# Chunked latent attention on one core: rope scores as two 128-row products instead of three 64-row ones

## The chip, the core and the metric

The kernel runs on one core of a Trainium2 chip. The metric is the device time of one execution in microseconds (us); less is better. Three runs of the kernel before took 1628.82, 1629.12 and 1631.48 us (median 1629.12). Engines are named as in the profile: PE is TensorE, PEld its weight loads, DVE VectorE, ACT ScalarE, POOL GpSimd, SP SyncE. L12 is line 12 of the kernel file.

## The reference

Two transformer blocks in float32 on 512 tokens of width 1024. The first block has an mLSTM layer and then a layer with latent attention; the second block is a pooling and differential attention layer with cross attention and an MLP. The change lies in the latent attention of the first block, 8 heads, cut to what matters:

```python
q = rmsnorm((rmsnorm(q_lat) @ w_q_up).reshape(b, s, 8, 192), q_gain)   # 128 nope + 64 rope columns
q = concat([q[..., :128], rope(q[..., 128:], positions)])
for j in range(4):                                   # blocks of 128 queries
    sc = einsum("bqhd,bkhd->bhqk", q[:, 128*j:128*j+128], k[:, :128*(j+1)]) * 192 ** -0.5
    sc = where(k_chunk <= q_chunk, sc, -inf)         # chunks of 64
    p = softmax(sc)
    out[j] = einsum("bhqk,bkhd->bqhd", p, v[:, :128*(j+1)])
```

The rope part of k (64 columns) is the same for all heads; the scale of q and the per-head scale of k are applied after the products.

## The kernel before, in words

Every float32 operand of a matmul is kept as two float32r tiles, hi and lo (`split`: ACT rounds, DVE subtracts, L534 to L540), and a product is three matmuls, hi by hi, hi by lo and lo by hi (`mm3`, L518). Weights come in slabs by SP's DMA and are split in four pieces each by an ACT and a DVE instruction (L285, L286; scaled ones L292, L293).

The program is a list of units. A unit's matmuls are emitted first; what follows a product (its `post`) is emitted when the next unit begins (`flush`, L451), ahead of which or behind which pieces of the weight slabs are put out: two when a slab begins, one or two for each unit after. All engines run in the order in which the units emit. So the order of units is the order of every engine's queue.

Latent attention handles the 8 heads in four groups of two. `prep(g)` makes the operands of a group: the nope part of k for each head (`kn`), sums of squares (`kss`), the rope part of q of both heads side by side in one 128-row tile (`qr`, rows 0 to 63 head 0, rows 64 to 127 head 1), the nope parts of q (`qn`), the row of k scales through DRAM to a broadcast tile `rkb` (`krow`: a transposition, ACT's copy `rr`, POOL's DMAs `rd` and twice `rkb`), the rotation (`qrot`: two PE products with a permutation, then three DVE operations L1265 to L1267 and a split), sums of squares of q (`qss`: products with one or two columns), and v (`vu`). The rope part of k, `Rk`, is rotated once and lies in both halves of its 128 rows.

`attend(g)` has 8 score tiles (2 heads, 4 query blocks): `f1` makes the scores (three matmuls nope, three matmuls rope with 64 rows, one bf16 mask product, width n = 256, 256, 384, 512), then on DVE the scaled maximum over the row (L1496, which reads `rkb`), `nb` (L1498), on ACT the exponential (L1499). `f2` is DVE's reciprocal and scaling to `e` (L1505, L1506). `f3` transposes e on PE and splits it into `PTh`, `PTl`. `f4` is the product with v (`po`), which reads PTh and PTl of all four blocks of its head, then `ym` and the split into y.

`soft_steps` lays the tiles of a group out in 11 steps: step i has f2 of tile i-1, f1 of tile i, then filling units, then f4 (steps 6 and 10), then f3 of tile i-2. The filling units come from `weave`, which spreads them evenly:

```python
for i, (before, after) in enumerate(steps):
    to = (len(main) * (i + 1)) // len(steps)
    res += before + main[m:to] + after
```

While group g attends, the filling units are `prep(g+1)` without v and the output product of the group before; `vu` follows behind the last step. Group 3 has only output products to fill in. The operands of group 0 are made ahead of everything, in an order written out by hand (L1544).

Of the kernel before, what the change touches and what calls it, by code (L numbers as in the profile page):

```python
# [26 lines left out]
def block_kernel(ctx: ExitStack, tc: tile.TileContext, A: dict, out: bass.AP, stop=None):  # L27
# [1225 lines left out]
        split(h, l, ps, scale=gain)  # L1253
        return ps, h, l, gain

    def rope_rotate(st, cosT, sinT, dst):
        ps, h, l, gain = st
        pr = bank([128, 512], "rot")
        pe.matmul(out=pr, lhsT=prm, rhs=h, start=True, stop=False)
        pe.matmul(out=pr, lhsT=prm, rhs=l, start=False, stop=True)  # L1260
        a, b = T("ra"), T("rb")
        if gain is None:
            dve.tensor_tensor(out=a, in0=ps, in1=cosT, op=ALU.mult)
        else:
            dve.scalar_tensor_tensor(out=a, in0=ps, scalar=gain, in1=cosT, op0=ALU.mult, op1=ALU.mult)  # L1265
        dve.tensor_tensor(out=b, in0=pr, in1=sinT, op=ALU.mult)
        dve.tensor_tensor(out=a, in0=a, in1=b, op=ALU.add)  # L1267
        split(dst[0], dst[1], a)

    mq1, mz0, mz1 = fmu(*bmq[1]), fmu(*bmz[0]), fmu(*bmz[1])  # L1270
    add(mq1, mem_q_ssq(0), mz0, U(rope_tables), mem_q_ssq(1), mz1)
# [116 lines left out]
    def prep(g):  # L1388
        kvb = w_kv_b[:, 512 * g:512 * g + 512].rearrange("(k p) (h c) -> p k h c", p=128, h=2)
        kkey, vkey = ("kvbk", g), ("kvbv", g)  # L1390
        for key, c in ((kkey, 0), (vkey, 128)):
            slabs[key] = ([(128 * h, kvb[:, :, h, c:c + 128]) for h in range(2)], 2, 256, ("kv_lat_norm", 0))
        qkey = ("qup", g)
        parts = []
        for i in range(2):
            src = b_w_q_up[:, 384 * g + 192 * i:384 * g + 192 * i + 192].rearrange("(k p) c -> p k c", p=128)
            parts += [(128 * i, src[:, :, 0:128]), (256 + 64 * i, src[:, :, 128:192])]
        slabs[qkey] = (parts, 3, 384, ("b_q_lat_norm", 0))

        def kn(h):  # L1400
            def post(ps):
                sq = H["ksq", g, h] = T("sq")
                act.activation(out=sq, in_=ps, func=AF.Square)
                k = H["kn", g, h] = pair(bh.p, [128, 512], "kn", bufs=3)
                split(k[0], k[1], ps, scale=g_nope)

            return fmu(kkey, 128 * h, post, src="cT", nk=2)

        def kss(h):
            def fn():  # L1410
                if h == 0:
                    H["kss", g] = bank([128, 2, 4], "ssk")
                sq = H.pop(("ksq", g, h))
                for tb in range(4):
                    pe.matmul(out=H["kss", g][:, h, tb:tb + 1], lhsT=sq[:, tb * 128:tb * 128 + 128], rhs=ones, start=True, stop=True)
                if h == 1:
                    sk = tiny(8, "fac").rearrange("p (a b) -> p a b", a=2)
                    dve.tensor_tensor(out=sk, in0=H.pop(("kss", g)), in1=S["ssp"].unsqueeze(1).to_broadcast([128, 2, 4]), op=ALU.add)
                    H["rk", g] = rsqrt(sk.rearrange("p a b -> p (a b)"), 8, 1.0 / 192)

            return U(fn)

        def krow():
            pr = bank([8, 128], "rkT")
            pe.transpose(out=pr, in_=H.pop(("rk", g)), identity=ident)
            rr = T("rr")[0:8, 0:128]
            act.copy(out=rr, in_=pr)
            rd = dram.tile([8, 128], F32, tag="rd", name="rd")
            pool.dma_start(out=rd, in_=rr)
            for h in range(2):  # L1430
                rb = H["rb", g, h] = bh.p.tile([128, 512], F32, tag="rkb", name="rkb", bufs=3)
                pool.dma_start(out=rb, in_=rd[4 * h:4 * h + 4, :].rearrange("a b -> (a b)").rearrange("(o c) -> o c", o=1).to_broadcast([128, 512]))

        def vu(b):
            def fn(w):
                if b == 0:
                    H["V", g] = pair(bh.p, [128, 4, 256], "V")
                ps = bank([128, 2, 256], "V")
                for i in range(2):
                    tm(ps[:, i], S["cT"], 2 * b + i, w, 0, 256, nk=2)  # L1440
                V = H["V", g]
                return lambda: split(V[0][:, 2 * b:2 * b + 2, :], V[1][:, 2 * b:2 * b + 2, :], ps)

            return U(fn, vkey)

        def qr_post(ps):
            sq = H["qsq", g] = [T("sq")]
            act.activation(out=sq[0], in_=ps, func=AF.Square)
            H["qrs", g] = rope_split(ps, col("b_q_gain", 1))

        def qrot():
            q = H["qr", g] = pair(bh.p, [128, 512], "qr", bufs=2)
            rope_rotate(H.pop(("qrs", g)), S["cos"], S["sin"], q)

        def qn(h):
            def post(ps):
                sq = T("sq")
                H["qsq", g].append(sq)
                act.activation(out=sq, in_=ps, func=AF.Square)
                q = H["qn", g, h] = pair(bh.p, [128, 512], "qn", bufs=3)  # L1460
                split(q[0], q[1], ps)

            return fmu(qkey, 128 * h, post, src="qlT", nk=3)

        def qss():
            sp = bank([128, 4, 2], "ssq")
            sqs = H.pop(("qsq", g))
            for tb in range(4):
                t = slice(tb * 128, tb * 128 + 128)
                pe.matmul(out=sp[:, tb, :], lhsT=sqs[0][:, t], rhs=blk1, start=True, stop=False)  # L1470
                for h in range(2):
                    pe.matmul(out=sp[:, tb, h:h + 1], lhsT=sqs[1 + h][:, t], rhs=ones, start=False, stop=h == 1)
            H["cq", g] = rsqrt(sp.rearrange("p a b -> p (a b)"), 8, 1.0 / 192, post=192 ** -0.5)

        qr = fmu(qkey, 256, qr_post, src="qlT", nk=3)
        return ([kn(0), kss(0), kn(1), kss(1), qr, qn(0), qn(1), U(krow), U(qrot), U(qss)],
                [vu(0), vu(1)])

    def attend(g):
        s1, s2, s3, s4 = [], [], [], []  # L1480
        for h in range(2):
            hs = slice(64 * h, 64 * h + 64)
            for j in range(4):
                t = slice(128 * j, 128 * j + 128)
                w = 128 * (j + 1)

                def f1(h=h, hs=hs, j=j, t=t, w=w):
                    n = max(w, 256)
                    kn, qn, qr, Rk = H["kn", g, h], H["qn", g, h], H["qr", g], S["Rk"]
                    ps = bank([128, 512], "sc")  # L1490
                    mm3(ps[:, 0:n], (qn[0][:, t], qn[1][:, t]), (kn[0][:, 0:n], kn[1][:, 0:n]), True, False)
                    mm3(ps[:, 0:n], (qr[0][hs, t], qr[1][hs, t]), (Rk[0][hs, 0:n], Rk[1][hs, 0:n]), False, False)
                    pe.matmul(out=ps[:, t], lhsT=idb, rhs=m_chunk, start=False, stop=True)
                    e = T("e")[:, 0:w]
                    mx, nb, sm = (tiny(1, n_) for n_ in ("mx", "nb", "sm"))
                    dve.tensor_tensor_reduce(out=e, in0=ps[:, 0:w], in1=H["rb", g, h][:, 0:w], scale=1.0, scalar=-3e38, op0=ALU.mult, op1=ALU.max, accum_out=mx)  # L1496
                    c = H["cq", g][:, 2 * j + h:2 * j + h + 1]
                    dve.scalar_tensor_tensor(out=nb, in0=mx, scalar=-1.0, in1=c, op0=ALU.mult, op1=ALU.mult)  # L1498
                    act.activation(out=e, in_=e, func=AF.Exp, scale=c, bias=nb, accum_out=sm)  # L1499
                    H["e", h, j] = e, sm  # L1500

                def f2(h=h, j=j):
                    e, sm = H["e", h, j]
                    rc = tiny(1, "rc")
                    dve.reciprocal(out=rc, in_=sm)  # L1505
                    dve.tensor_scalar(out=e, in0=e, scalar1=rc, scalar2=None, op0=ALU.mult)  # L1506

                def f3(h=h, j=j):
                    e, _ = H.pop(("e", h, j))
                    pt = bank([128, 4, 128], "pt")  # L1510
                    for k in range(j + 1):
                        pe.transpose(out=pt[:, k, :], in_=e[:, 128 * k:128 * k + 128], identity=ident)
                    hi, lo = (pt_view(i, j) for i in range(2))
                    split(hi, lo, pt[:, 0:j + 1, :])

                s1.append(U(f1))
                s2.append(U(f2, early=True))
                s3.append(U(f3))
# [22 lines left out]

    preps = [prep(g) for g in range(4)]
    add(U(open_bh))
    add([preps[0][0][i] for i in (0, 2, 1, 4, 3, 5, 6, 7, 8, 9)], preps[0][1])  # L1544
    for g in range(4):
        m = outproj(f"oB{g - 1}", b_w_out, 2 * (g - 1), 2, slots=((g - 1) % 2,)) if g else []
        if g < 3:
# [689 lines left out]
```

## Time and profile before

| | us |
|---|---|
| three runs | 1628.82, 1629.12, 1631.48 |
| the profiled execution, its own time | 1630.76 |
| its span from first to last instruction | 1629.0 |
| PE busy | 1559.9 (96%) |
| PE weight loads busy | 1354.0 (83%) |
| DVE busy | 1071.3 (66%) |
| ACT busy | 743.3 (46%) |
| POOL busy | 312.5 (19%) |
| first score tile of group 0, last mask product of group 3 | from 662.5, 829.3 |

Busy time of PE counts matmuls from start to a modelled end, and matmuls overlap; so what a matmul costs is read from the distance between the starts of two. The latent attention, with the making of its first operands, lies between 645 and 844 us of the span.

### The profile page before, as it was taken

To read this page: it belongs to the slowest core of one execution; us is meant where nothing else is said; L and a number is where in the kernel's file an instruction comes from. 1 tells how busy PE (TensorE), PEld (TensorE's weight loads), DVE (VectorE), ACT (ScalarE), POOL (GpSimd) and SP (SyncE) were. 2 spreads that over 40 slices of the span, in tenths; PEclk is the share of its full clock that TensorE was granted. 3 is DMA by queue.
4 is the path that set the end of the run, shared out by engine and by line. 5 is a ranking of instruction groups with operands and counts; after the bars stand their busy time and mean duration, and the time that the engine had idled before them with its cause. 6 is when DMAs were issued, how large, how long until landed. Compare 5 with 4: busy or idle time off the path is not lost. (4 is left out here: it accounts for less than half of the span.)

```text
span 1629.0 us, 24253 instructions
## 1 busy us (share of the span) xinstructions
PE 1559.9 (96%) x9385; PEld 1354.0 (83%) x9385; DVE 1071.3 (66%) x1980; ACT 743.3 (46%) x1538; POOL 312.5 (19%) x570
## 2 busy tenths in 40 slices
PE   6999999999999999999989999989999999999996
PEld 6889898988788888778869877868878889898986
DVE  6567646565685563667777555577456579686968
ACT  5344424333465544445544333455333463636353
POOL 4100000000030100211211000012100265555552
PEclk9999999999999999999999999999999999999998
DMA  8422223221332221212324331233312224141411
GB/s 265 140 78 70 87 78 90 67 92 65 129 112 83 91 78 35 92 35 67 124 72 148 116 118 52 73 109 117 99 70 73 76 85 156 52 156 52 142 53 52
DMA packets 134795, 152.75 MB, mean 94 GB/s; under 512 B 7616, under 2 KB 120024, under 8 KB 134680
## 3 DMA queue, kind: packets, MB, share of 16 engines
q1 hardware_dynamic: 131800, 143.58, 27.7%
q0 software_dynamic: 2304, 6.57, 1.4%
q8 instruction: 74, 1.21, 0.3%
q10 hardware_dynamic: 576, 1.05, 0.2%
q14 instruction: 41, 0.34, 0.1%
HBM read 144.88 MB, written 6.31 MB: 93 GB/s over the span
## 5 line engine op out<-in xcount | busy, mean ns | idle before, releaser
L520 PE MATMUL fm<-xth,whi 128*128 128x512 f32 (+1 forms) x824 | 307.3, 373 | 1.0 <-ACT whi L285 0.8
L521 PE MATMUL fm<-xtl,whi 128*128 128x512 f32 (+1 forms) x824 | 305.9, 371 | 1.5 <-DVE xtl L537 1.5
L522 PE MATMUL fm<-xth,wlo 128*128 128x512 f32 (+1 forms) x824 | 305.0, 370 | 0.1
L286 DVE TENSOR_TENSOR wlo<-wraw,whi 128x512 fp32r<-128x512 f32 (+2 forms) x324 | 206.3, 680 | 32.8 <-ACT whi L285 23.3
L285 ACT ACTIVATE whi<-wraw 128x512 fp32r<-128x512 f32 (+2 forms) x324 | 182.7, 619 | 38.8 <-PE op L522 23.3
L521 PEld LDWEIGHTS fm<-xtl,whi 128*128 128x128 f32 x824 | 156.0, 189 | 28.8 <-DVE xtl L537 2.5
L520 PEld LDWEIGHTS fm<-xth,whi 128*128 128x128 f32 x824 | 155.9, 189 | 28.4 <-ACT whi L285 1.0
L522 PEld LDWEIGHTS fm<-xth,wlo 128*128 128x128 f32 x824 | 155.7, 189 | 27.9 <-DVE wlo L286 0.5
L547 POOL TENSOR_TENSOR rsx<-rsy 128x1 f32<-128x1 f32 (+2 forms) x49 | 15.1, 307 | 753.8 <-DVE rsy L546 707.7
L520 PE MATMUL tm<-whi,xth 128*128 128x256 f32 x416 | 116.4, 280 | 0.0
L521 PE MATMUL tm<-wlo,xth 128*128 128x256 f32 x416 | 115.8, 278 | 0.0
L522 PE MATMUL tm<-whi,xtl 128*128 128x256 f32 x416 | 115.7, 278 | 0.0
L669 DVE TENSOR_TENSOR xall<-op,xall 128x512 f32<-128x512 f32 x120 | 81.7, 686 | 47.3 <-PE op L522 47.0
L522 PE MATMUL dn<-whi,ffgl 128*128 128x256 f32 x296 | 82.8, 280 | 0.0
L521 PE MATMUL dn<-wlo,ffgh 128*128 128x256 f32 x296 | 82.7, 279 | 0.0
L520 PE MATMUL dn<-whi,ffgh 128*128 128x256 f32 x296 | 82.6, 279 | 0.0
L521 PEld LDWEIGHTS tm<-wlo,xth 128*128 128x128 f32 x416 | 78.7, 189 | 0.2
L520 PEld LDWEIGHTS tm<-whi,xth 128*128 128x128 f32 x416 | 78.7, 189 | 0.2
L522 PEld LDWEIGHTS tm<-whi,xtl 128*128 128x128 f32 x416 | 78.7, 189 | 0.0
L520 PE MATMUL op<-whi,y0h 128*128 128x512 f32 x160 | 66.8, 417 | 0.0
L522 PE MATMUL op<-whi,y0l 128*128 128x512 f32 x160 | 64.0, 400 | 0.0
L521 PE MATMUL op<-wlo,y0h 128*128 128x512 f32 x160 | 63.8, 399 | 0.0
(590 smaller groups left out, 4038.5 us busy)
## 6 DMA issues: line engine op xcount, KB each, us to landing
wraw<-in_a_w_in_dram SPq DMA_DIRECT2D x23, 1024.0 KB
wraw<-in_w_down_dram SPq DMA_DIRECT2D x19, 512.0 KB
wraw<-in_mem_w_kv_dram SPq DMA_DIRECT2D x8, 1024.0 KB
wraw<-in_b_w_in_dram SPq DMA_DIRECT2D x8, 1024.0 KB
wraw<-in_w_ckv_dram SPq DMA_DIRECT2D x8, 1024.0 KB
wraw<-in_w_in_dram SPq DMA_DIRECT2D x8, 1024.0 KB
wx<-in_w_down_dram SPq DMA_DIRECT2D x13, 512.0 KB
wraw<-in_a_w_out_dram SPq DMA_DIRECT2D x6, 1024.0 KB
```

Of the source, the lines that this page charges most:

```text
L285: act.activation(out=hi[:, s], in_=t[:, s], func=AF.Copy)
L286: dve.tensor_tensor(out=lo[:, s], in0=t[:, s], in1=f(hi)[:, s], op=ALU.subtract)
L520: pe.matmul(out=ps, lhsT=lh, rhs=rh, start=first, stop=False)
L521: pe.matmul(out=ps, lhsT=lh, rhs=rl, start=False, stop=False)
L522: pe.matmul(out=ps, lhsT=ll, rhs=rh, start=False, stop=last)
L547: eng.tensor_tensor(out=x, in0=y, in1=y, op=ALU.mult)
L669: return lambda: dve.tensor_tensor(out=xs[tb][h], in0=ps, in1=xs[tb][h], op=ALU.add)
```

## The change

The three 64-row rope products of a score tile become two of 128 rows. For a head h, `qr[h]` is now one 128-row tile that holds the hi part of the head's 64 rope rows in one half and the lo part in the other. Since Rk has the same 64 rows in both halves, one product with Rk hi gives (hi + lo) by hi, and one with Rk lo gives (hi + lo) by lo. The rotation writes its hi part into the tile `rph` and its lo part into the tile `rb`, and a new unit `qmove` copies the four 64-row pieces of a group into the two tiles `qr[0]`, `qr[1]` by four DMAs on ACT's queue (from SBUF to SBUF, 64 rows of 2 KB each, 128 KB).

`qmove` is one more unit at the end of each `prep`. So groups 1 and 2 spread 19 filling units over 11 steps in place of 18, group 0 spreads 7 over its last 5 steps in place of 6, and the list written by hand for the first operands has the rotation ahead of the second nope part of q, and `krow` behind `qmove`.

```diff
-    def rope_rotate(st, cosT, sinT, dst):
+    def rope_rotate(st, cosT, sinT, dst=None):
         ps, h, l, gain = st
         pr = bank([128, 512], "rot")
         pe.matmul(out=pr, lhsT=prm, rhs=h, start=True, stop=False)
         pe.matmul(out=pr, lhsT=prm, rhs=l, start=False, stop=True)
-        a, b = T("ra"), T("rb")
+        a, bt = T("ra"), T("rb", F32R)
+        b = f(bt)
...
         dve.tensor_tensor(out=a, in0=a, in1=b, op=ALU.add)
+        dst = dst or (h, bt)
         split(dst[0], dst[1], a)
+        return dst
...
         def qrot():
-            q = H["qr", g] = pair(bh.p, [128, 512], "qr", bufs=2)
-            rope_rotate(H.pop(("qrs", g)), S["cos"], S["sin"], q)
+            H["qrp", g] = rope_rotate(H.pop(("qrs", g)), S["cos"], S["sin"])
+
+        def qmove():
+            hl = H.pop(("qrp", g))
+            q = H["qr", g] = [bh.p.tile([128, 512], F32R, tag=f"qr{h}", name="qr", bufs=2) for h in range(2)]
+            for h in range(2):
+                for i in range(2):
+                    d = 64 * (h ^ i)
+                    nc.scalar.dma_start(out=f(q[h])[d:d + 64, :], in_=f(hl[i])[64 * h:64 * h + 64, :])
...
-        return ([kn(0), kss(0), kn(1), kss(1), qr, qn(0), qn(1), U(krow), U(qrot), U(qss)],
+        return ([kn(0), kss(0), kn(1), kss(1), qr, qn(0), qn(1), U(krow), U(qrot), U(qss), U(qmove)],
                 [vu(0), vu(1)])
...
                     mm3(ps[:, 0:n], (qn[0][:, t], qn[1][:, t]), (kn[0][:, 0:n], kn[1][:, 0:n]), True, False)
-                    mm3(ps[:, 0:n], (qr[0][hs, t], qr[1][hs, t]), (Rk[0][hs, 0:n], Rk[1][hs, 0:n]), False, False)
+                    for r in Rk:
+                        pe.matmul(out=ps[:, 0:n], lhsT=qr[h][:, t], rhs=r[:, 0:n], start=False, stop=False)
                     pe.matmul(out=ps[:, t], lhsT=idb, rhs=m_chunk, start=False, stop=True)
...
-    add([preps[0][0][i] for i in (0, 2, 1, 4, 3, 5, 6, 7, 8, 9)], preps[0][1])
+    add([preps[0][0][i] for i in (0, 2, 1, 4, 3, 5, 8, 6, 10, 7, 9)], preps[0][1])
```

## Rows read from the trace of the kernel before

**Rows 1.** Windows: us, PE, PEld, DVE, ACT, POOL busy, clock, DMA, GB/s
```profile
640.00:840.00 200.00, 193.16 (x1028) 154.84 (x1026) 135.53 (x355) 94.42 (x216) 33.66 (x114) 0.96 0.25 75
706.00:709.00 3.00, 3.00 (x12) 2.81 (x12) 2.27 (x4) 0.63 (x1) 0.80 (x2) 0.50 0.68 178
803.20:844.00 40.80, 36.63 (x183) 28.09 (x182) 29.69 (x82) 17.63 (x43) 10.05 (x30) 0.90 0.36 112
```

**Rows 2.** Timeline of PE in the first score tile: start, us, engine, line, what
```profile
662.73 0.28 PE L522 MATMUL sc<-knh,qnl 128*128 128x256 f32 x1
662.94 0.38 PE L520 MATMUL sc<-Rkh,qrh 64*128 64x256 f32 x1
663.17 0.27 PE L521 MATMUL sc<-Rkl,qrh 64*128 64x256 f32 x1
663.28 0.28 PE L522 MATMUL sc<-Rkh,qrl 64*128 64x256 f32 x1
663.49 0.23 PE L1493 MATMUL sc<-masks,idb 128*128 128x128 bf16 x1
663.53 0.48 PE L520 MATMUL fm<-cTh,whi 128*128 128x512 f32 x1
```

**Rows 3.** Instructions on score tiles: ns min/median/max, first and last start, forms
```profile
L522 PE MATMUL sc<-Rkh,qrl x32: 273/305/393, 663.3 to 829.0; 64*128 64x256 f32 x16, 64*128 64x384 f32 x8, 64*128 64x512 f32 x8
```

**Rows 4.** Timeline of PE at the end of group 1
```profile
748.51 0.39 PE L522 MATMUL fm<-qlTh,wlo 128*128 128x512 f32 x1
...
748.85 0.60 PE L1512 MATMUL pt<-ident,e 128*128 128x128 f32 x4
...
752.36 0.47 PE L520 MATMUL po<-PTh,Vh 128*128 128x512 f32 x1
753.27 0.57 PE L521 MATMUL po<-PTl,Vh 128*128 128x512 f32 x1 [0.44 <-DVE PTl L537]
```

**Rows 5.** Timeline of DVE at the end of group 1
```profile
748.31 0.55 DVE L537 TENSOR_TENSOR PTl<-pt,PTh 128x384 fp32r<-128x384 f32 x1
750.12 0.69 DVE L537 TENSOR_TENSOR qnl<-fm,qnh 128x512 fp32r<-128x512 f32 x1 [1.26 <-ACT qnh L536]
750.73 1.89 DVE L286 TENSOR_TENSOR wlo<-wraw,whi 128x512 fp32r<-128x512 f32 x3
752.53 0.68 DVE L537 TENSOR_TENSOR PTl<-pt,PTh 128x512 fp32r<-128x512 f32 x1
...
753.73 0.74 DVE L1265 SCALAR_TENSOR_TENSOR ra<-fm,cols,cosT 128x512 f32<-128x512 f32 x1
...
757.11 0.16 DVE L567 TENSOR_SCALAR rsv<-ssq 128x8 f32<-128x8 f32 x1
```

**Rows 6.** Timeline of PE at the end of group 0
```profile
701.97 0.63 PE L1512 MATMUL pt<-ident,e 128*128 128x128 f32 x4 [1.53 <-DVE e L1506]
```

**Rows 7.** Timeline ahead of group 0: DVE, ACT, ACT, POOL, DVE, PE
```profile
655.19 0.69 DVE L537 TENSOR_TENSOR qnl<-fm,qnh 128x512 fp32r<-128x512 f32 x1 [1.66 <-ACT qnh L536]
...
656.17 0.60 ACT L1459 ACTIVATE sq<-fm 128x512 f32<-128x512 f32 x1 [1.02 <-PE fm L522]
...
657.94 0.24 ACT L1427 COPY rr<-rkT 8x128 f32<-8x128 f32 x1
...
660.38 1.14 POOL L1432 DMA_DIRECT2D rkb<-rd  x2 [1.32 <-DMA rd<-rr]
...
665.15 0.28 DVE L1496 CUSTOM_DVE_ANT_0 e<-sc,rkb 128x128 f32<-128x128 f32 x1
...
668.27 0.51 PE L521 MATMUL op<-wlo,y1h 128*128 128x512 f32 x1 [0.23 <-DVE wlo L286]
```

**Rows 8.** DMA issues, 640 to 662.5: count, KB each, us to landing
```profile
rkb<-rd POOLq DMA_DIRECT2D x2, 256.0 KB, 4.3
```

**Rows 9.** DMA issues of the last line of the kernel: ns minimum, median, maximum
```profile
L2158 ACTq DMA_DIRECT2D out_dram<-xall x4: 343/410/464, 1622.4 to 1624.6; - x4
```

**Rows 10.** Timeline of PE at the end of group 3
```profile
836.19 1.11 PE L1512 MATMUL pt<-ident,e 128*128 128x128 f32 x4 [2.54 <-DVE e L1506]
```

More of the change, by code (lines that the diff above doesn't have):

```diff
@@ L1481, in attend @@
         for h in range(2):
-            hs = slice(64 * h, 64 * h + 64)
             for j in range(4):
@@ L1485, in attend, with f1 @@
                 w = 128 * (j + 1)
-                def f1(h=h, hs=hs, j=j, t=t, w=w):
+                def f1(h=h, j=j, t=t, w=w):
                     n = max(w, 256)
```

## The prediction

> **What bounds the kernel now.** I read the windows first: in the stretch that the change touches, PE is busy 193 of 200 us and DVE 136 [rows 1], so PE is the bound on average, but the last 41 us (group 3) are not like that: PE is idle there for 4.2 us and granted 0.90 of its clock. Then the timeline of PE for one score tile, because a product's price is the distance between starts. Then, at the ends of the groups, the timelines of PE and DVE side by side, because the change moves the rotation there; and last the way of the k scales ahead of group 0. The reader is to see that PE gains something in every tile, that at the group ends DVE's queue ends last, and that the one queue that gets new work (ACT's) stands in the way of group 0's first softmax.
>
> **Score tiles.** Two neighbouring rope products start 0.11 us apart (663.17 to 663.28). But the first starts 0.21 after the last nope product, the second 0.23 after the first, and the mask product 0.21 after the third [rows 2]. So three of the steps cost about 0.1 us more than the work; all three lie where the row count goes from 128 to 64 or back, or just behind it. With 128 rows throughout I take every step at 0.115: from the last nope product to the unit behind the mask 0.39 us (three steps and the mask's 0.04) in place of 0.80, a saving of 0.41 for 256 columns. A 512-column product is 0.12 longer than a 256-column one, a 384-column one about half of that [rows 3]; so 16 tiles save 0.41, 8 save 0.47, 8 save 0.53: 14.6 us for 32 tiles, 3.64 a group.
>
> Here a rule speaks against me. The rows show the 0.1 us steps at each change of the row count. The Trainium skill (TensorE: Matmul & The Clock Gate, section Why this matters for your kernels) says that a single product over few rows takes the same time as one over 128, which leaves only the third product as a gain. By it the saving would be 32 steps of 0.11 to 0.23, 4.9 us; by the rows it is 14.6. I take the rows, and keep the rule as a rival.
>
> **Group 3 keeps nothing.** It has little to fill in, and PE waits there for softmax results, 2.54 us before its last transpositions [rows 10]. Its chain runs from DVE's maximum over ACT's exponential to DVE again; shorter score products lengthen PE's waits. I take 0 of its 3.64 (bounds 0 and -3.64). So the tiles are worth -10.9 in groups 0 to 2.
>
> **The rotation ahead of the last transpositions.** With one more unit, the spread puts `qrot` into step 9 and `qss`, `qmove` into step 10. The transpositions of tile 7 come at the end of step 9. So the rotation, which stood behind them, now stands ahead of them on all three engines: DVE's PTl of tile 7 waits behind ra, rb, the sum, ACT's hi and DVE's lo. And the value product of step 10 needs PTl. From ra to the operation behind the lo part DVE needs 757.11 - 753.73 = 3.38 us, an ACT turn included [rows 5].
>
> Group 1, from the end A of the second nope part of q (748.75, one step of 0.24 after 748.51 [rows 4]). Before: DVE's split of it at A+1.37, three weight pieces (0.60 each), PTl at A+3.8, second value product at 753.27, A+4.5. After: the spread puts both nope parts into step 8, ahead of the transpositions of tile 6. DVE then has behind A: the split (A+1.37 to A+1.98), four weight pieces (2.4) and PTl of tile 6 (0.47), so ra at A+4.8 and PTl of tile 7 at A+8.2; with its 0.65 and PE's start the second value product comes at A+8.9. PE itself would be there at A+3.9 (3.5 from the transpositions to the value product, rotation included [rows 4], and 0.35 for those of tile 6 and the row of k scales): it waits some 5 us. A lies 0.24 earlier, as tile 6's transpositions now follow it. Loss 8.9 - 4.5 - 0.24 = 4.1. Group 2 has the same units: 4.1. In group 0 the four weight pieces and tile 6 already stood ahead of PTl, so only the 3.4 are added; the wait of 1.53 us for e [rows 6] comes from DVE and ACT too and gives nothing back. Sum 11.6. Bounds: if DVE came to ra as soon as the rotation product is there, the chain of 4.1 would stand against 3.0 of PE work (the 3.5 without the rotation), 1.1 less what PE waits now, 1.5 for three groups; 13.5 if the pieces are dearer.
>
> **The four moves.** An issue on ACT costs 0.41 us [rows 9], 1.64 for four, 16 in all. At the group ends ACT has nothing urgent behind them (y and v come later). They land 4.3 us after issue if they behave like the 256 KB broadcasts [rows 8]; from the wait's end PE has the rest of the value products, 24 v products and three nope products, 38 steps of 0.115 at least, 4.4 us, and the issue comes 0.7 before that. This just covers it: 0, bounds 0 and 1.5 a group. The tiles rph and rb are held until the moves land; they are reused 8 allocations later, in the next group's first tiles: 0 while those 4.4 us hold.
>
> **Ahead of group 0.** Now rr, the first link to `rkb`, stands behind the moves on ACT. DVE splits the first nope part at 655.19 [rows 7]; ra follows 0.6 later, 655.8, ACT's hi 2.1 later (ra, rb and the sum), 657.9, then the square of the second nope part at 658.45, then as before 1.77 to where rr stood (656.17 to 657.94), and 1.64 for the moves: rr at 661.9, 3.9 late. POOL's DMAs move with it: `rkb` issued at 664.3 instead of 660.38, landed at 668.6 [rows 8], when DVE's first maximum started at 665.15. Behind this maximum stand on DVE the weight pieces for which PE already waits at 668.27 [rows 7]. So PE goes on about 3.3 us later than before, and the 0.8 that it saved in two tiles are swallowed: +4.1 against the tiles' sum. `qss` also waits for that square, under the same wait. Bounds: -0.4 (the landing hidden, and `krow` no longer waiting for POOL) and 6.
>
> **Clock.** Behind the waits at the group ends PE already runs at half clock (0.50 from 706 to 709) and loses 1.7 us in 3.4; those falls stay. New waits ahead of group 0 may bring one more: +0.7, bounds -3 and 5.
>
> Sum: -10.9 + 11.6 + 4.1 + 0.7 = +5.5. The profiled execution took 1630.76 us, 1.64 above the median of the runs, so 1636.3 on its own scale and 1634.6 on that of the median.
>
> **Rivals.** (A) Faster: DVE reaches the rotation without delay, so the ends cost 1.5 and not 11.6. This decides between gain and loss: up to a start of ra about 1.4 us behind the rotation product instead of 4, the tiles win. Then -10.9 + 1.5 + 4.1 + 0.7 = -4.6: 1624.5; with `rkb` hidden too, 1620. For it: DVE is busy only 136 of 200 us. Against: its queue is in order, with four weight pieces ahead. 0.22. (B) No change: `rkb` is hidden, -0.4 in place of 4.1, and the ends cost as forecast: +1.0, 1630. For it: some slack in the landing. Against: DVE took the first maximum 0.5 us after the landing reckoned by these rows. 0.16. (C) Moves land late and the clock falls for longer: 1.5 in each of three groups and 2 more for the clock, +12, 1641. The Trainium skill (the same page, section HAM oscillation) says that pauses between bursts of products bring the half clock back, and the trace agrees with 0.50 behind such an end. 0.08. (D) The row change is not what costs the 0.1 us steps, so the change does not do what it says: the 24 tiles of three groups give one product each, 0.11, 0.17 or 0.23 by width, 3.7 in place of 10.9: +12.7, 1641.8. The rule on few rows above would have it so. Against: rows 2. 0.06. The forecast has 0.48, its own range 1631 to 1639.
>
> **Numbers.** 0.2% (3.3 us) is about what a measurement can tell. Faster: A with 0.21, the lower edge of B and of the forecast 0.03: 0.24. Same: most of B (0.12) and the forecast's lower part (0.05): 0.17. Slower: 0.59. The range 1622.5 to 1640.5 leaves out the far part of A, and most of C and D.
>
> **What would show it.** Right: rope products at the common step, no 0.2 us starts; at the ends of groups 0 to 2 the L1265 to L1267 operations ahead of the 512-wide PTl, and PE waiting 3 us or more for PTh or PTl at a po product; the first L1496 at 668 or later. Wrong: po products that start without such a wait, a first L1496 near 665, or score tiles whose first rope product still starts late.

## The result, and the profile after

The changed kernel is slower: 1638.76 us (1638.33 to 1643.89, 4 runs) against 1630.30 us (1628.82 to 1632.17, 4 runs), ratio 1.0059 with a 95% interval of 1.0035 to 1.0082. Run again beside two of the experiments it took 1639.65 against 1631.44, ratio 1.0050 (1.0035 to 1.0065). The forecast was 1634.6 with a range of 1622.5 to 1640.5, and slower as the likeliest.

The execution that was profiled first took 1643.89 us, 5.1 over the slowest of the three others. So most rows below are of the second trace, taken when the kernel ran again (1640.04 us, 9.3 over the profiled execution of before); the first one serves where the two differ. Their largest difference in the stretch of the change is 2.9 us ahead of group 0.

First the page of the second trace, its span and busy times:

```profile
span 1638.3 us, 24225 instructions
...
PE 1552.4 (95%) x9353; PEld 1354.1 (83%) x9353; DVE 1072.9 (65%) x1980; ACT 742.5 (45%) x1538; POOL 312.0 (19%) x570
```

PE has 32 products fewer and is busy 7.5 us less (1559.9 before), and still the end is 9.3 us later: the change gave work back and added waiting. The window of [rows 1] and the stretch ahead of group 0, second trace; the last line is that stretch in the first trace:

```profile
640.00:840.00 200.00, 179.56 (x973) 150.20 (x972) 126.14 (x331) 88.62 (x200) 29.03 (x100) 0.92 0.29 84
...
655.00:675.00 20.00, 17.37 (x96) 14.53 (x96) 11.06 (x27) 8.66 (x18) 6.62 (x23) 0.91 0.45 134
...
655.00:675.00 20.00, 17.92 (x89) 16.19 (x87) 8.49 (x20) 7.29 (x16) 5.95 (x23) 0.74 0.43 125
```

PE is now idle for 20.4 of 200 us, where it was idle for 6.8, and its granted clock fell from 0.96 to 0.92. What it waits for is told by the view of waits of PE, 640 to 860 (engine, operation, line, released by: us in total, times, longest); the first fence is before, the second the changed kernel's second trace:

```profile
PE pt L1512 <- DVE e L1506: 4.6, 3, 2.5
PE po L520 <- ACT PTh L536: 0.7, 1, 0.7
```

```profile
PE po L520 <- ACT PTh L536: 11.8, 4, 4.0
PE pt L1524 <- DVE e L1518: 9.1, 7, 2.5
PE ssq L1484 <- ACT sq L1471: 2.1, 1, 2.1
```

The value products wait for PTh, 11.8 us in place of 0.7; the transpositions wait twice as long for e; a wait for a square is new; none is for a moved tile qr. Now the score tile that answers to [rows 2], timeline of PE, second trace:

```profile
670.29 0.28 PE L522 MATMUL sc<-knh,qnl 128*128 128x256 f32 x1
670.40 0.28 PE L1504 MATMUL sc<-Rkh,qr 128*128 128x256 f32 x1
670.52 0.28 PE L1504 MATMUL sc<-Rkl,qr 128*128 128x256 f32 x1
670.64 0.23 PE L1505 MATMUL sc<-masks,idb 128*128 128x128 bf16 x1
670.68 0.47 PE L520 MATMUL op<-whi,y0h 128*128 128x512 f32 x1
```

Every step is 0.11 to 0.12, and from the last nope product to the unit behind the mask it is 0.39 us where it was 0.80. The end of group 1 on DVE and then on PE, the answer to [rows 5] and [rows 4]:

```profile
757.11 0.55 DVE L537 TENSOR_TENSOR PTl<-pt,PTh 128x384 fp32r<-128x384 f32 x1
757.58 1.28 DVE L286 TENSOR_TENSOR wlo<-wraw,whi 128x512 fp32r<-128x512 f32 x2
758.78 0.75 DVE L1267 SCALAR_TENSOR_TENSOR ra<-fm,cols,cosT 128x512 f32<-128x512 f32 x1
...
761.60 0.69 DVE L537 TENSOR_TENSOR rb<-ra,rph 128x512 fp32r<-128x512 f32 x1 [0.76 <-ACT rph L536]
762.21 0.68 DVE L537 TENSOR_TENSOR PTl<-pt,PTh 128x512 fp32r<-128x512 f32 x1
762.81 0.16 DVE L567 TENSOR_SCALAR rsv<-ssq 128x8 f32<-128x8 f32 x1
```

```profile
753.17 0.39 PE L522 MATMUL fm<-qlTh,wlo 128*128 128x512 f32 x1
754.90 0.63 PE L1524 MATMUL pt<-ident,e 128*128 128x128 f32 x4 [0.43 <-DVE e L1518]
762.11 0.80 PE L520 MATMUL po<-PTh,Vh 128*128 128x512 f32 x1 [4.01 <-ACT PTh L536]
762.95 0.79 PE L521 MATMUL po<-PTl,Vh 128*128 128x512 f32 x1
```

The rotation, ra to the lo part in rb, stands ahead of the 512-wide PTl and takes 3.43 us (758.78 to 762.21). PE waits 4.01 us ahead of the first value product of step 10, which then runs at half clock (0.50 granted from 762 to 766): 0.80 us for a product that took 0.47 before [rows 4]. Ahead of group 0 (ACT, POOL, DVE, PE; compare [rows 7]):

```profile
660.07 0.63 ACT L536 ACTIVATE rph<-ra 128x512 fp32r<-128x512 f32 x1 [2.80 <-DVE ra L1269]
660.60 0.58 ACT L1471 ACTIVATE sq<-fm 128x512 f32<-128x512 f32 x1
...
663.27 0.26 ACT L1431 COPY rr<-rkT 8x128 f32<-8x128 f32 x1 [0.81 <-issue]
...
666.68 1.14 POOL L1436 DMA_DIRECT2D rkb<-rd  x2 [2.28 <-DMA rd<-rr]
...
669.37 1.31 DVE L286 TENSOR_TENSOR wlo<-wraw,whi 128x512 fp32r<-128x512 f32 x2
670.60 0.28 DVE L1508 CUSTOM_DVE_ANT_0 e<-sc,rkb 128x128 f32<-128x128 f32 x1
...
661.23 0.38 PE L1484 MATMUL ssq<-ones,sq 128*128 128x1 f32 x2 [2.08 <-ACT sq L1471]
```

PE has nothing left when it comes to the sums of squares: the square stands on ACT behind rph, which waited 2.80 us for the rotation's sum on DVE. The copy rr and the rkb transfers are late as forecast, but DVE's first maximum starts straight behind two weight pieces with no wait of its own.

The table gives the lengths of five stretches, each from its first product on PE to the next one's (from the first k product of group 0; each group from its first score product; the last to the transpositions behind group 3):

| us | ahead of group 0 | group 0 | group 1 | group 2 | group 3 | sum |
|---|---|---|---|---|---|---|
| before | 17.58 | 49.55 | 47.38 | 47.32 | 36.37 | 198.20 |
| changed order alone, 64-row products (experiment 2) | 20.85 | 52.82 | 51.54 | 51.41 | 36.20 | 212.82 |
| changed, first trace | 23.75 | 51.10 | 49.78 | 48.90 | 35.96 | 209.49 |
| changed, second trace | 20.89 | 52.34 | 48.79 | 49.92 | 35.38 | 207.32 |
| direct halves, old order (below) | 17.58 | 52.05 | 42.35 | 44.25 | 37.59 | 193.82 |
| direct halves, changed start, old ends (below) | 23.27 | 49.36 | 43.93 | 43.82 | 36.67 | 197.05 |
| direct halves, old start, changed ends (below) | 17.59 | 53.34 | 50.35 | 49.20 | 37.01 | 207.49 |

The 9.1 us of the second trace lie ahead of group 0 (3.3) and in groups 0 to 2 (2.8, 1.4, 2.6); group 3 gained 1.0. Each row is one execution, and the two of the changed kernel differ by up to 1.2 us in a group and by 2.9 ahead of group 0, so a difference of 1 or 2 us between two rows is not shown by them alone.

### The profile page after: what moved, and what is told of

Same layout as the page of the kernel before. It is cut to its first block, busy times and chain, and to the rows that moved or that the text cites. A ratio compares the mean times of both kernels' runs of the same rounds, so it can differ in the third digit from the quotient of the medians.

```text
span 1641.9 us, 24225 instructions
## 1 busy us (share of the span) xinstructions
PE 1560.4 (95%) x9353; PEld 1362.6 (83%) x9353; DVE 1072.1 (65%) x1980; ACT 742.4 (45%) x1538; POOL 309.2 (19%) x570
## 4 chain that ended last, share of the span: by engine, by line
PE 41%; DVE 8%; ACT 4%; issue 3%; POOL 2%; DVEq 0%; ACTq 0%; POOLq 0%
PE fm L521 6%; PE fm L520 6%; PE fm L522 6%; PE dn L522 3%; PE dn L521 3%; PE dn L520 3%; PE op L520 2%; PE op L521 2%; PE op L522 2%; DVE wlo L286 1%; PE po L521 1%; DVE PTl L537 1%; PE po L522 1%; PE ck L521 0%; ACT junk L582 0%
```

## The experiments

All times stand beside runs of the kernel before on the same chip: 1628.53 us for the first four, 1630.58 for the next four, 1630.26 and 1631.44 for the last two pairs. Where letters stand in the first expectations, O is the theory that the order costs (the early rotation), M that the moves do, and S that the tiles save only their third product.

**1. The old order put back, the moves kept.** Three kernels: the ends alone, the start alone, both. The edits, ends first:

```diff
-        return ([... U(krow), U(qrot), U(qss), U(qmove)],
-                [vu(0), vu(1)])
+        return ([... U(krow), U(qrot), U(qss)],
+                [U(qmove), vu(0), vu(1)])
...
-    add([preps[0][0][i] for i in (0, 2, 1, 4, 3, 5, 8, 6, 10, 7, 9)], preps[0][1])
+    add([preps[0][0][i] for i in (0, 2, 1, 4, 3, 5, 6, 7, 8, 9, 10)], preps[0][1])
```

> The changed kernel, with the rotation again behind the last transpositions of a group (the moves stand ahead of the v products, outside the spread); the start stays as changed. Theory O (the order of units costs it: rotation ahead of the last PTl at three group ends, square of the second nope part behind the rotation at the start): the waits of 4 us for PTh go, and about 11 us with them: 1628 us, up to 1632 if the moves now land late (they are issued some 2 us before the first rope product needs them). Rival M (the moves themselves cost it: their issue on ACT, their landing, their traffic): within 2 us of 1638.8, or slower. Rival S (the score tiles save only the third product, 4 us instead of 11): as O for this kernel.

> The changed kernel with the first operands in the order of before and the moves at the end of that list; the group ends stay as changed. Theory O: PE's 2.1 us wait for the square and the half clock over qss and the 24 v products go, 5.6 us: 1633 us (the 5.6 is what the trace of the changed kernel lost up to the third score tile). Rival M: no change, 1638 to 1639. Rival S: as O.

> Both at once: 128-row scores and moves, order of units as before the change, moves ahead of the v products. Theory O: before less the tiles' 10.9: 1620 us if the moves are hidden, 1624 if PE waits 1 to 1.5 us for them in each group. Rival M: 1636 or more. Rival S: 1630.3 less 3.7 and plus the landing, 1627 to 1630.

Measured: ends 1635.32 (1.0043, 1.0028 to 1.0058), start 1643.15 (1.0088, 1.0073 to 1.0103), both 1638.93 (1.0068, 1.0051 to 1.0085). None came near what theory O gives, the third lies where rival M has it. Timeline of PE, two of the four rope products that wait in the kernel with both put back (groups 0 and 3), and on ACT's queue the last move ahead of the second one:

```profile
667.18 0.58 PE L1504 MATMUL sc<-Rkh,qr 128*128 128x256 f32 x1 [4.30 <-DMA qr<-rb]
...
816.84 0.55 PE L1504 MATMUL sc<-Rkh,qr 128*128 128x256 f32 x1 [4.55 <-DMA qr<-rb]
...
812.44 0.62 ACTq L1465 DMA_DIRECT2D qr<-rb  x1
```

With the old order the four moves land too late: in this kernel PE waits 12.0 us in four places for them, with only the ends put back 9.2 in three, with only the start 5.3 in one. In group 3 the last issue began at 812.44, and the product started at 816.84, 4.4 us later. So the early rotation, whose price experiment 2 shows, is also what hides the moves.

**2. The order alone, with the old score products.** Before's kernel, its 64-row products and no moves, with an empty unit and the changed list:

```diff
-        return ([... U(krow), U(qrot), U(qss)],
+        return ([... U(krow), U(qrot), U(qss), U(lambda: None)],
...
-    add([preps[0][0][i] for i in (0, 2, 1, 4, 3, 5, 6, 7, 8, 9)], preps[0][1])
+    add([preps[0][0][i] for i in (0, 2, 1, 4, 3, 5, 8, 6, 10, 7, 9)], preps[0][1])
```

> The kernel before with the changed order alone: an empty unit in the place of the moves and the changed order of the first operands, scores of three 64-row products, no DMA added. Theory O: slower by the changed kernel's 8.5 and the tiles' 10.9 together, 1649 us, with the PTh waits at the group ends. Rival M: 1630 to 1632. Rival S: 1630.3 plus 8.5 plus 3.7, 1642.

1648.17, ratio 1.0122 (1.0101 to 1.0144), as theory O has it. The waits of PE:

```profile
PE po L520 <- ACT PTh L536: 10.4, 4, 4.0
PE ssq L1472 <- ACT sq L1459: 2.0, 1, 2.0
```

The order alone costs 19.6 us, with the waits for PTh and for the square, and without a single move. The table above gives this kernel's stretches: 3.3 us more than before ahead of group 0, 3.3, 4.2 and 4.1 more in groups 0 to 2, 0.2 less in group 3. The prediction had 4.1, and 3.4, 4.1 and 4.1. The traced execution took 1645.16 us; the four lie in two pairs, at 1645.2 and 1651.1, and the upper pair has no trace.

**3. The tiles without moves, and the order taken apart.** The two halves of a head's tile are written where they belong by ACT (hi, same rows) and by DVE (lo, 64 rows further down or up):

```diff
-        split(dst[0], dst[1], a)
+        for q, d in ((fresh[0], 0), (fresh[1], 64)):
+            act.activation(out=q[d:d + 64, :], in_=a[d:d + 64, :], func=AF.Copy)
+        for q, d in ((fresh[0], 0), (fresh[1], 64)):
+            dve.tensor_tensor(out=q[64 - d:128 - d, :], in0=a[d:d + 64, :], in1=f(q)[d:d + 64, :], op=ALU.subtract)
```

With the old order at both places; with the changed start; with the changed ends (the empty unit); with both.

> The changed score tiles (two products of 128 rows) with the order of the kernel before at the start and at the ends, and no moves: ACT writes the two hi halves, and DVE the two lo halves, straight into the tile of each head, in halves of 64 rows (one operation more of 0.6 us on each of the two engines per group). The tiles alone. Theory of the prediction (row change costs, groups 0 to 2 keep 10.9, less up to 0.6 at each of three ends): 9 to 11 us under the kernel before, 1618 to 1621; no wait of PE for a tile qr and no wait of 4 us for PTh. Rival, only the third product counts: 3.7 us under it, 1625 to 1626. Rival, the tiles are hidden by waits elsewhere: within 2 us of the kernel before.

> As the kernel with direct halves in the old order, but ahead of group 0 the rotation stands ahead of the second nope part of q, as in the changed kernel; still no moves. If the square behind the rotation on ACT is what made the start late (PE waits for it 2 us and then runs at half clock): 4 to 6 us above its twin with the old start, 1623 to 1627, with a wait of about 2 us of the ssq product for sq. If the moves on ACT ahead of the copy rr were what made it late: within 1 us of its twin, 1619 to 1621, and no such wait.

> As the kernel with direct halves in the old order, old start, but with an empty unit more in each group, so that the rotation of groups 0 to 2's ends stands ahead of the last transpositions as in the changed kernel; no moves. Theory of the prediction: 3.4, 4.1 and 4.1 us more than its twin, 10 to 14 us, 1630 to 1634, with waits of about 4 us of a value product for PTh at the ends of groups 1 and 2. Rival, the order costs only because the moves' issues stand on ACT with it: within 3 us of its twin, 1619 to 1623.

> The changed order at the start and at the ends together, with direct halves in place of the four moves: the changed kernel without its moves. If the moves cost nothing where they are covered (step of the prediction): as the changed kernel or up to 3 us above it, since two 64-row operations take the place of one on DVE ahead of the last transpositions (0.7 us at each of three ends): 1638 to 1643, ratio to the kernel before 1.005 to 1.008. If the moves' issues on ACT (0.5 us each, 16) lie on the path: 4 to 8 us under the changed kernel, 1631 to 1635.

| direct halves | us | ratio to before (95%) |
|---|---|---|
| old order | 1625.25 | 0.9968 (0.9956 to 0.9979) |
| changed start | 1630.97 | 1.0000 (0.9990 to 1.0010) |
| changed ends | 1639.61 | 1.0061 (1.0046 to 1.0076) |
| changed start and ends | 1643.11 | 1.0078 (1.0055 to 1.0101) |

The first beats both kernels, by 5.3 us and by some 14; it is the version to keep. The start costs 5.7 us without a single move (timeline of PE, kernel with the changed start):

```profile
658.75 0.38 PE L1478 MATMUL ssq<-ones,sq 128*128 128x1 f32 x2 [2.81 <-ACT sq L1465]
```

So it is the square behind the rotation, not the moves' issues ahead of rr. The ends cost 14.4 us, a little over the 10 to 14 expected; two halves on DVE in place of one operation, 0.7 us more at each of three ends, are 2.1 of that by estimate. The changed kernel, with moves in place of halves, is 8.5 and 8.2 us over the kernel before, its twin without moves 12.9, which is some 4.5 more and not the up to 3 expected. The extra halves, 0.7 us at the start and at three ends, would account for 2.8 of that; the rest stays open. Where the early rotation covers them, the moves cost nothing that shows.

But the tiles, with their extra halves, gave 5.3 us and not the 9 to 11 expected; by the time alone that is nearer to the 3.7 of the third product, and experiment 4 decides between the two. The table above tells where: groups 1 and 2 became 5.0 and 3.1 us shorter, group 0 became 2.5 longer, and group 3 1.2 longer. With the changed start and the same tiles and ends, groups 1 and 2 became 3.4 and 3.5 shorter, group 0 0.2 shorter and group 3 0.3 longer. What both show is that groups 0 and 3 keep nothing. The end of group 0 on DVE, first the kernel before and then the one with direct halves:

```profile
700.21 0.69 DVE L537 TENSOR_TENSOR qnl<-fm,qnh 128x512 fp32r<-128x512 f32 x1 [2.00 <-ACT qnh L536]
...
701.34 0.49 DVE L1506 TENSOR_SCALAR e<-e,rc 128x512 f32<-128x512 f32 x1
```

```profile
700.51 0.69 DVE L537 TENSOR_TENSOR qnl<-fm,qnh 128x512 fp32r<-128x512 f32 x1 [2.00 <-ACT qnh L536]
701.12 0.41 DVE L537 TENSOR_TENSOR PTl<-pt,PTh 128x256 fp32r<-128x256 f32 x1
...
701.64 0.49 DVE L1512 TENSOR_SCALAR e<-e,rc 128x512 f32<-128x512 f32 x1
```

PE's wait there (compare [rows 6]), with the old start and then with the changed one:

```profile
702.27 0.63 PE L1518 MATMUL pt<-ident,e 128*128 128x128 f32 x4 [2.93 <-DVE e L1512]
...
704.90 0.63 PE L1518 MATMUL pt<-ident,e 128*128 128x128 f32 x4 [2.93 <-DVE e L1512]
```

DVE has the same 2.00 us wait for qnh in both kernels and scales this e 0.30 us later, though group 0 began 0.82 later: DVE and ACT set this end, and shorter tiles mostly made PE wait 2.93 us for e in place of 1.53. The granted clock then falls for longer. The windows behind it, before and then with direct halves:

```profile
706.00:720.00 14.00, 14.00 (x76) 11.96 (x76) 9.28 (x25) 5.72 (x12) 3.45 (x12) 0.89 0.35 100
```

```profile
706.00:720.00 14.00, 14.00 (x72) 13.04 (x73) 8.83 (x21) 4.47 (x9) 3.75 (x12) 0.73 0.33 98
```

PE is busy throughout in both, at 0.89 and at 0.73: 2.2 us of full speed less in 14.

**4. What in the tile costs.** Before's kernel without its third rope product (query lo by key hi is left out):

```diff
-                    mm3(ps[:, 0:n], (qr[0][hs, t], qr[1][hs, t]), (Rk[0][hs, 0:n], Rk[1][hs, 0:n]), False, False)
+                    for r in Rk:
+                        pe.matmul(out=ps[:, 0:n], lhsT=qr[0][hs, t], rhs=r[hs, 0:n], start=False, stop=False)
```

> The kernel before with the third rope product of every score tile left out (query lo times key hi is not computed), so two products of 64 rows. If the change of row count costs 0.1 us each time: steps of 0.2 us stay at the first rope product, at the second and at the mask, a 256-wide tile gets shorter by 0.11 only, 3 to 4 us in all, 1625 to 1627, far from the kernel with direct halves. If the third product is what the change saves (rival D): the same time as the kernel with direct halves.

1628.03, ratio 0.9985 (0.9975 to 0.9995): 2.6 us under the kernel before, a little less than expected, and 2.8 over the kernel with direct halves. Timeline of PE:

```profile
665.17 0.28 PE L522 MATMUL sc<-knh,qnl 128*128 128x256 f32 x1
665.38 0.38 PE L1493 MATMUL sc<-Rkh,qrh 64*128 64x256 f32 x1
665.61 0.28 PE L1493 MATMUL sc<-Rkl,qrh 64*128 64x256 f32 x1
665.81 0.23 PE L1494 MATMUL sc<-masks,idb 128*128 128x128 bf16 x1
665.85 0.47 PE L520 MATMUL op<-whi,y0h 128*128 128x512 f32 x1
```

The steps of 0.21, 0.23 and 0.20 stay; the tile takes 0.68 from the last nope product. Of the 0.41 that the change saves here, 0.12 is the product and 0.29 the change of the row count. So theory S and rival D fall by the steps. Of the 9.3 us that 0.29 would make in 32 tiles, 2.8 appear between the two kernels' times: groups 0 and 3 keep nothing, and what the extra halves cost was not separated.

**5. The end of group 0.** An attempt to better the version with direct halves: group 1's rope product of q and its nope parts one step earlier.

```diff
-                add(weave(a0[0:6], ... + ob[7:8] + p[3:4]), weave(a0[6:], p[4:]), preps[1][1])
+                add(weave(a0[0:6], ... + ob[7:8] + p[3:5]), weave(a0[6:], p[5:8] + [U(lambda: None)] + p[8:]), preps[1][1])
```

> The kernel with direct halves in the old order, with the rope product of group 1's query one step earlier and so both nope parts one step earlier at the end of group 0, to free DVE and ACT there (PE waited 2.9 us for e of the last tile). If the nope part's split, for which DVE waits 2 us ahead of the scaling of e, is what holds the end of group 0: PE's wait there falls to under 1.5 us and the time by 1 to 3 us, 1622 to 1624. If it only moves the wait to the step before: within 1 us of its twin, 1624 to 1626.

A miss: 1629.45, ratio 0.9996 (0.9985 to 1.0008). PE's wait for that e is 5.16 us in place of 2.93: on DVE two weight pieces (1.28 us) now stand between the second nope part's split and the scaling of e, and the first nope part's split stands ahead of y. The wait for ACT stays.

**6. The moves doubled.** The changed kernel again, and one with each move issued twice:

```diff
-                    nc.scalar.dma_start(out=f(q[h])[d:d + 64, :], in_=f(hl[i])[64 * h:64 * h + 64, :])
+                    for _ in range(2):
+                        nc.scalar.dma_start(out=f(q[h])[d:d + 64, :], in_=f(hl[i])[64 * h:64 * h + 64, :])
```

> The changed kernel itself, for a trace whose time lies nearer to its median (the first one was 5.1 us above its three other executions) and beside its twin with the moves issued twice: 1637 to 1641, ratio to the kernel before 1.004 to 1.008; of the time from the first k product of group 0 to the transpositions behind group 3, 8 to 12 us more than before.

> The changed kernel with each of the four moves of a group issued twice in a row. If the moves' issues on ACT and their landing are covered (step of the prediction, 0): within 1.5 us of the changed kernel, 1637 to 1642, no wait for qr. If the issues lie on the path (four more of 0.5 us per group ahead of the k scales, of y and of v): 6 to 8 us above the changed kernel, 1644 to 1648. If the landing becomes late with twice the bytes: waits of PE for qr of 1 us or more at the first tiles, 1641 to 1646.

1639.65 and 1677.90 (1.0293, 1.0274 to 1.0311). All three expectations for the doubled moves were wrong, because the edit does more than double: the same half is written twice, and by the rows below the second issue is held until the first has landed while ACT's queue stands. Timeline of ACT and its queue ahead of group 0:

```profile
657.29 0.52 ACTq L1466 DMA_DIRECT2D qr<-rph  x1
...
659.54 0.54 ACTq L1466 DMA_DIRECT2D qr<-rph  x1
660.12 4.07 ACTq L1466 DMA_DIRECT2D qr<-rb  x2
664.22 2.84 ACTq L1466 DMA_DIRECT2D qr<-rph  x2
667.10 3.53 ACTq L1466 DMA_DIRECT2D qr<-rb  x2
670.67 0.25 ACT L1431 COPY rr<-rkT 8x128 f32<-8x128 f32 x1 [11.65 <-DMA qr<-rb]
```

The run does not price an issue. It prices a wait on ACT's queue: 11.65 us ahead of rr. How ACT's issues would price alone was not tried in another way.

## Why the prediction was right

The sign, the place and the number hold (1634.6 forecast, 1638.76 measured, in the range; +5.5 forecast, +8.5 and +8.2 measured), but the terms do not all hold. By the traces the tiles gave 5 to 6 us less than forecast and the order cost 1 to 2 us less (14.6 against 15.7, or 16.4 with the clock), so two misses of opposite sign partly cancel. By the medians the effects measured one at a time do not add up: -5.3, 14.4 and 5.7 make 14.8, the three together measured 12.9, and 8.5 with moves in place of halves. So that the sum came within 3 us is in part luck.

- **Tiles in groups 0 to 2, -10.9: mis-sized.** The step lengths were right (0.39 for a tile, as worked out). What failed is that group 0 was counted as keeping them. The step on the rotation already said that its wait for e "comes from DVE and ACT too and gives nothing back"; that holds for the tiles as well. Measured: -5.3 in all, with direct halves in the old order. In the changed order the worth of the tiles is not settled: between the order alone and the changed kernel it is 11.2 by the medians, but 4.7 and 6.0 by groups 0 to 2 of the changed kernel's two traces.
- **Group 3 keeps nothing: right.** It changed by -0.4 and -1.0 in the two traces, and PE waits 2.54 us at its last transpositions as in [rows 10].
- **Rotation ahead of the last transpositions, +11.6: right in mechanism and size.** With the old products 11.5 in the stretches of groups 0 to 2 (experiment 2); with direct halves 14.4 between the medians of the two kernels that differ in it alone, 12.3 without the estimated 2.1 of the extra halves, the clock included. DVE stood in the order forecast; PE waited 4.0 us in groups 1 and 2, and 2.7 in group 0, under the 3 that the prediction named as a sign.
- **Ahead of group 0, +4.1: right size, wrong reason.** The prediction led the delay over rr and rkb to DVE's first maximum. It was the square for `qss`, named there only as standing under the same wait. The sign named for it, a first maximum at 668 or later, came true (670.60) without being the cause. The wait for the square costs 3.3 us in the second trace and with the order alone, and 5.7 between the medians of the kernels with and without it; in the first trace 6.2, with the clock of 655 to 675 at 0.74 where the second had 0.91.
- **Moves, 0: right where the rotation is early, and only there.** An issue took 0.54 to 0.56 us in the median, not 0.41, at no visible cost. With the old order they cost 6 to 16 us: taken each against the kernel before beside it, the kernels of experiment 1 lie 6.4 (ends put back), 5.6 (start put back) and 15.7 us (both) above their twins with direct halves.
- **Clock, +0.7: mis-sized.** Over 640 to 840 the granted clock went from 0.96 to 0.92 (0.90 in the first trace), 8 us of full speed less in 200. Some of that lies in waits and costs nothing; how much was not separated.

Rival A (no delay at the ends) falls with the 4.0 us waits for PTh. B (rkb hidden) is right in that DVE's first maximum did not wait for rkb, but the square held PE up. C has its clock but not its late moves. D, by the rule of the Trainium skill (TensorE: Matmul & The Clock Gate, section Why this matters for your kernels) that a product over few rows takes as long as one over 128, falls in experiment 4: single products are indeed equally long here (0.28 us for the second of 64 rows and for those of 128; the first of 64 rows is drawn at 0.38), and yet the tile keeps 0.29 us more than the rule would leave.

## What to carry to other kernels

A saving on the busiest engine counts only in the stages that this engine sets: read at each stage's end which queue comes last, and give a stage that ends on another queue nothing. A unit put into an evenly spread list moves its neighbours too, here past the transpositions, and that cost more than twice what the tiles gave. When data must change partitions, see first whether the engine that writes it can write it there; a DMA needs a place in which its landing is covered, and the order that makes this place has its own price.

## What the runs showed of the hardware

DVE wrote rows 0 to 63 of its operands to rows 64 to 127 and back, and a 64-row operation takes as long as one of 128 rows (timeline of DVE, direct halves):

```profile
708.88 0.69 DVE L1274 TENSOR_TENSOR qr<-ra,qr 64x512 fp32r<-64x512 f32 x1 [0.70 <-ACT qr L1272]
```

Going from 128 rows to 64 and back cost 0.29 us in a tile of width 256, in three starts that each came about 0.1 us late: the first 64-row product, the second one, and the first of 128 rows behind them (0.21, 0.23 and 0.20 us in place of 0.115). The moves of 128 KB from SBUF to SBUF needed from 2.25 us (the first of the doubled ones, from its issue to the issue that waited for it) to 4.4 us (group 3 of experiment 1, from the last issue to the product that waited for it). And two executions of one kernel differed by 2.9 us in the stretch ahead of group 0, with granted clocks of 0.74 and 0.91 there behind the same wait of 2.08 us.
